# A two-block network on one core: one-hots made in fours and scaled by ScalarE, row products spaced wider, V gathers issued later, attention by pairs of heads

## The chip, the cores and the metric

The kernel runs on one core of a Trainium2 chip. The metric is the device time of one execution in microseconds, the median of three runs. One more execution was taken by the hardware profiler; its trace has the start and duration of every instruction on the engines (PE is TensorE's products, PEld its weight loads, DVE VectorE, ACT ScalarE, POOL GpSimd, SP SyncE, which issues most transfers), each transfer, and the clock that TensorE was granted.

## The reference

Two blocks on 512 tokens of width 1024, all in float32. The first mixes tokens (a gated delta rule and dilated attention) and then applies a PEER layer; the second has two layers, each with a mixer of three kinds (gated linear attention, neighbourhood attention, sliding-window attention, the last two also over 256 context tokens) and a SwiGLU. What the change touches is PEER and the two softmax attentions:

```python
def peer_ffn(xn, w_q, sub_keys, expert_u, expert_v):
    scores = einsum('thcd,hckd->thck', (x2 @ w_q)..., sub_keys)      # 8 heads, 2 halves, 128 keys
    sv, si = top_k(scores, 16)
    cv, ci = top_k(sv[..., 0, :, None] + sv[..., 1, None, :], 16)    # of 256 pairs
    experts = i1 * 128 + i2                                          # 128 experts a token, of 16384
    gates = softmax(cv)
    act = gelu(einsum('tkd,td->tk', expert_u[experts], x))
    return einsum('tk,tkd->td', act * gates, expert_v[experts])
...
s = concat([q k_loc^T * scale + bias, q k_ctx^T * scale (, sink)])   # 6 heads of 64 in each attention
o = softmax(s) @ concat([v_loc, v_ctx])
```

## The kernel before, in words

**Exact products.** Most products are made of three passes over operands split in two parts (`mm3`, L204 to L206: hi x hi, hi x lo, lo x hi). A weight tile of 128 x 1024 is loaded by SP (tile wr), its high part is made by ScalarE (wh, L142), its low part by VectorE (wl, L199). Other products are plain float32; the trace shows each as two records.

**PEER in two ways.** For 384 of the 512 tokens the layer is computed densely: H = gelu(x U^T) for all 16384 experts, in 128 blocks of 24 products of 384 columns (`peer_h`, tile h, stored to DRAM as Hd); a matrix G of gates for every expert and token, made from one-hots (`peer_g`, stored as Gd); then the output as (H * G) V, in 128 blocks of 18 products of 512 columns (`peer_v`). For the first 128 tokens, rows are gathered instead: `sparse_u` gathers a row of U for each of 128 expert places (GpSimd, 128 rows of 4 KB at a time, into a ring of six buffers, four of them slices of x) and VectorE makes the row product (L931), four gathers ahead; when all 128 are there and the gates are known, gelu and gates are applied and the result is transposed; then `sparse_v` gathers rows of V, four gathers a step, 32 steps, each with eight products of 32 weight columns in four column strips (L956).

**G.** A G step (`peer_g`) treats four tokens. One VectorE instruction makes the one-hots of the first key for all four (tile oa, two buffers). For the second key, one VectorE instruction a token compares and multiplies by the gate (L993, tile ob, four buffers of one token). A product a token (L995) gives its 128 x 128 gates in a quarter of a PSUM bank, ScalarE copies the bank to gs. There are 96 G steps.

**The order of the work.** `interleave` writes the instructions of several lanes in one order. It keeps a planned time; each lane yields a pair (planned TensorE time, wait until it is due again), or a condition. The first lane that is due goes next; a spare lane (here `peer_h`, in half-blocks of planned 2.1 us, always due) fills when none is. The order so written is the priority; the framework then places instructions on each engine, and may put a ready one before one whose operands are late. During the selection the lanes are `peer_select` (top 16 of scores, of pairs, and the look-up of indices, nearly all VectorE) and `sparse_u` (a gap of 1.7 a row product). Then, under the mark H+G, `peer_g` (0.9, 1.5) and the first 12 turns of `sparse_v` (2.0, 12.0; one turn is the wait for the row products, so 11 steps). What is left of H follows, and then the V stage with the rest of `sparse_v` beside the dense blocks (4.1, 0). The buffers of the first two V blocks are in a pool that is open from the start; the others use room that the H stage gives back.

**Attention.** In `mixers` the lanes are GLA, three lanes that take attention units from a queue, and the projections. A unit (`attn_unit`) is one head and 128 queries: scores to PSUM, softmax over VectorE and ScalarE (L386 to L396), four or five transposes (two in the context mixer), a copy to SBUF, and the product with V (L410) of 64 weight columns into the head's half of the partitions. `softmax` and `probs_times_v` pause twice a unit (3.2 and 0.9). The mixer runs for the context of the first layer (256 tokens) and for the tokens of both layers (512 each); a further one for the context of the second layer has no attention.

Of the kernel before, what the change touches and what calls it, by code (L numbers as in the profile page):

```python
# [23 lines left out]
CTX = 256  # L24
# [81 lines left out]
class Net:  # L106
# [812 lines left out]
    def sparse_u(s, S):  # L919
# [6 lines left out]
        for k in range(128 + 4):  # L926
            if k < 128:
                ahead.append(s.gather(S, s.I["Ur"], S["rows"][:, k:k + 1]))
            if k >= 4:
                g = ahead.pop(0)  # L930
                nc.vector.tensor_tensor_reduce(g, g, S["xt"], scale=1.0, scalar=0.0, op0=ALU.mult, op1=ALU.add,  # L931
                                               accum_out=act[:, k - 4:k - 3])
                yield 0.0, 1.7
# [8 lines left out]
    def sparse_v(s, S):  # L942
# [7 lines left out]
        for t in range(32):  # L950
# [8 lines left out]
            yield 2.0, 12.0  # L959
# [65 lines left out]
    def peer_hg(s, st, x, Hd, Gd, S, keep):  # L1025
# [27 lines left out]
        with ExitStack() as t:  # L1053
# [134 lines left out]
    def gla(s, p, T, L, pair, s0, sout, y):  # L1188
# [9 lines left out]
        for d in range(2):  # L1198
# [21 lines left out]
            if y is not None:  # L1220
                qin = s.t(p, "gqi", [128, T], 1)
# [90 lines left out]
    def attn_unit(s, p, q, loc, ctx, sink, vs, po, after=None):  # L1312


        mm = s.nc.tensor.matmul
        lw = loc[2] if loc else 0
        b0 = s.bank()
        cps = b0[:, lw:lw + CTX] if lw + CTX <= 512 else s.bank()[:, :CTX]
        segs = [(cps, s.zero[:, 0:1].to_broadcast([128, CTX]), lw)]
        if loc:  # L1320
            mm(b0[:, :lw], q, loc[0], start=True, stop=False)  # L1321
            mm(b0[:, :lw], q, loc[1], start=False, stop=True)
            segs.append((b0[:, :lw], loc[3](), 0))
        mm(cps, q, ctx[0], start=True, stop=False)
        mm(cps, q, ctx[1], start=False, stop=True)
        pr = s.t(p, "pr", [128, 640], 3)
        s.softmax(pr, segs, sink)
        yield (lw + CTX) * 2 * COL, 3.2
        yield from s.probs_times_v(p, pr, vs, po())
        if after:  # L1330
            after()

    def layer_consts(s, p, i):
        s.glan, s.sink = s.t(p, "glan", [128, 16], 1)[:, :2], s.t(p, "sink", [128, 16], 1)[:, :6]
# [35 lines left out]
    def mixers(s, st, i, T, xp, xh, xl, y, is_ctx, lanes=()):  # L1370
# [9 lines left out]
        def units(kind, n, make):  # L1380
# [36 lines left out]
        def na_units(pair, ks, vw, qs, ck):  # L1417
            def mk(po, after):
                for n in range(nt):
                    nb = None  # L1420
                    if not is_ctx:
                        nb = {}
                    for h in range(2):
                        hh = slice(64 * h, 64 * h + 64)
                        cv = [KV["nv"][:, j, pair * 128 + 64 * h:pair * 128 + 64 * h + 64] for j in range(2)]
                        o = lambda n=n, hh=hh: po()[hh, n * 128:(n + 1) * 128]
                        q = qs[h][:, n * 128:(n + 1) * 128]
                        if is_ctx:
                            yield s.attn_unit(p, q, None, ks[h], None, cv, o, after)
                            continue  # L1430
                        w0 = (0, 64, 192, 256)[n]

                        def bias(n=n, h=h, nb=nb):
                            if "t" not in nb:
                                nb["t"] = s.t(p, "nbias", [128, 2, 256], 2)
                                nc.sync.dma_start(nb["t"], s.I["nabias"][i, n, :, 2 * pair:2 * pair + 2, :])
                            return nb["t"][:, h]
                        vs = [vw[:, n, j, hh] for j in range(2)] + cv
                        yield s.attn_unit(p, q, (ks[h][0][:, w0:w0 + 256], ks[h][1][:, w0:w0 + 256], 256, bias),
                                          ck[h], None, vs, o, after)  # L1440
            return mk

        def swa_units(pair, ks, vt, qs, ck):
            def mk(po, after):
                for n in range(nt):
                    for h in range(2):
                        head = 2 * pair + h
                        kv = head // 3
                        hh, vh = slice(64 * h, 64 * h + 64), slice(64 * kv, 64 * kv + 64)
                        cv = [KV["sv"][:, j, vh] for j in range(2)]  # L1450
                        q = qs[h][:, n * 128:(n + 1) * 128]
                        o = lambda n=n, hh=hh: po()[hh, n * 128:(n + 1) * 128]
                        sk = s.sink[:, head:head + 1]
                        if is_ctx:
                            yield s.attn_unit(p, q, None, ks[kv], sk, cv, o, after)
# [3 lines left out]
                        yield s.attn_unit(p, q, (ks[kv][0][:, lo * 128:hi * 128], ks[kv][1][:, lo * 128:hi * 128], w,  # L1459
                                                 lambda c0=c0, w=w: s.c2["swam"][:, c0:c0 + w]), ck[kv], sk,  # L1460
                                          [vt[:, j, vh] for j in range(lo, hi)] + cv, o, after)
# [4 lines left out]
        def proj_lane():  # L1466
            for kind, m in seq:
# [3 lines left out]
                if kind in ("nk", "sq") and y is not None:  # L1471
                    left = aq.put_pairs - 2
                    yield lambda left=left: aq.done >= left * 2 * nt
# [48 lines left out]
                elif kind == "nq":  # L1522
                    pair = m - 9
                    qs = s.q_parts(p, s.evac(p, ps, "ra", T, bufs=2, scale=0.125, grid=not is_ctx), T, "qp")
                    units(kind, 2 * nt, dict(units=na_units(pair, A["k"], A["v"], qs, A.get("ck")),
# [425 lines left out]
```

## Time and profile before

| | us |
|---|---|
| median of three runs (4079.09 to 4084.34) | 4083.6 |
| profiled execution, its own time | 4080.38 |
| its span, first to last instruction | 4078.6 |
| TensorE busy | 3921.0 (96%) |
| VectorE busy | 2324.0 (57%) |
| ScalarE busy | 1573.6 (39%) |
| GpSimd busy | 325.7 (8%) |

The kernel moves 637.62 MB, 156 GB/s over the span; in the PEER part it is near 300. The mean granted clock is 0.988. In lists of groups the columns are line, engine, operation, tiles, shapes, count, busy time, mean ns of one, idle time of the engine before them and what ended it. Busy times of TensorE overlap, as a product starts before the one ahead of it ends.

### The profile page before, as it was taken

What the parts mean: (1) busy time and instruction counts of PE and PEld (TensorE: products, weight loads), DVE (VectorE), ACT (ScalarE), POOL (GpSimd) and SP (SyncE); (2) the same over time, 40 slices, a digit from 0 to 9 for tenths busy, and PEclk for the clock granted to TensorE, in tenths of its full rate; (3) what the DMA queues carried; (4) which work ended last, traced back from release to release, by engine and by line L of the source; (5) the groups of instructions that cost most, each with busy time, mean ns of one, the idle gap of its engine ahead of it and who ended that gap; (6) DMA issues with size and microseconds to landing.
All of it is one profiled execution on the core that took longest, in us unless ns stands there. A gap on an engine that the chain in (4) does not pass through costs nothing.

```text
span 4078.6 us, 57929 instructions
## 1 busy us (share of the span) xinstructions
PE 3921.0 (96%) x22491; PEld 3316.5 (81%) x22491; DVE 2324.0 (57%) x5133; ACT 1573.6 (39%) x2776; POOL 325.7 (8%) x287
## 2 busy tenths in 40 slices
PE   8999999999878999989998999999999999999998
PEld 5878988789877899766887778888888888887887
DVE  7526544569998776434556757663222266664334
ACT  5335454433223333323333645553121245553222
POOL 0000000004445310222000000000000000000000
PEclk9999999999998999999999999999999999999999
DMA  5342132338889876988764651121212141122332
GB/s 196 106 150 74 37 99 98 113 115 321 316 293 326 319 266 236 339 287 308 257 217 163 241 198 43 58 83 63 67 63 62 60 127 58 55 86 78 95 96 83
DMA packets 218594, 637.62 MB, mean 156 GB/s; under 512 B 25552, under 2 KB 65360, under 8 KB 214736
## 3 DMA queue, kind: packets, MB, share of 16 engines
q1 hardware_dynamic: 181456, 499.69, 36.3%
q0 software_dynamic: 36864, 134.23, 9.1%
q8 instruction: 177, 2.90, 0.3%
q14 instruction: 97, 0.79, 0.1%
HBM read 575.12 MB, written 58.72 MB: 155 GB/s over the span
## 4 chain that ended last, share of the span: by engine, by line
PE 54%; DMA 8%; DVE 6%; issue 1%; ACT 1%; POOL 0%; DVEq 0%; SPq 0%; ACTq 0%; POOLq 0%
PE ac L205 13%; PE ac L206 13%; PE ac L204 13%; DMA pa<-Hd 6%; PE po L410 3%; PE bk L995 2%; DVE wl L199 2%; PE bk L236 2%; PE bk L205 1%; PE bk L204 1%; PE bk L206 1%; DVE pl L145 1%; DMA wr<-V 1%; PE bk L1321 1%; PE bk L1165 1%
## 5 line engine op out<-in xcount | busy, mean ns | idle before, releaser
L204 PE MATMUL ac<-xh,wh 128*128 128x512 f32 (+2 forms) x3608 | 1301.6, 362 | 54.2 <-ACT h L136 41.2
L206 PE MATMUL ac<-xh,wl 128*128 128x512 f32 (+2 forms) x3608 | 1280.8, 356 | 14.1 <-DVE wl L199 13.8
L205 PE MATMUL ac<-xl,wh 128*128 128x512 f32 (+2 forms) x3608 | 1282.0, 356 | 1.0 <-DVE xl L148 0.7
L142 ACT ACTIVATE wh<-wr 128x1024 fp32r<-128x1024 f32 (+1 forms) x599 | 630.4, 1054 | 1618.9 <-PE ac L205 1173.4
L199 DVE TENSOR_TENSOR wl<-wr,wh 128x1024 fp32r<-128x1024 f32 (+1 forms) x599 | 726.9, 1214 | 557.4 <-ACT wh L142 529.8
L204 PEld LDWEIGHTS ac<-xh,wh 128*128 128x128 f32 x3608 | 683.8, 190 | 160.5 <-ACT h L136 51.7
L206 PEld LDWEIGHTS ac<-xh,wl 128*128 128x128 f32 x3608 | 683.8, 190 | 96.4 <-DVE wl L199 20.7
L205 PEld LDWEIGHTS ac<-xl,wh 128*128 128x128 f32 x3608 | 684.7, 190 | 79.8 <-issue 7.8
L145 DVE TENSOR_TENSOR pa<-pa,pg 128x384 f32<-128x384 f32 x128 | 66.1, 555 | 298.1 <-DMA pa<-Hd 292.0
L205 PE MATMUL bk<-wl,ph 128*128 128x512 f32 x512 | 201.2, 393 | 0.0
L204 PE MATMUL bk<-wh,ph 128*128 128x512 f32 x512 | 201.1, 393 | 0.0
L206 PE MATMUL bk<-wh,pl 128*128 128x512 f32 x512 | 200.6, 392 | 0.0
L205 PE MATMUL ac<-al,wh 128*128 128x512 f32 (+1 forms) x528 | 186.0, 352 | 0.0
L206 PE MATMUL ac<-ah,wl 128*128 128x512 f32 (+1 forms) x528 | 185.5, 351 | 0.0
L204 PE MATMUL ac<-ah,wh 128*128 128x512 f32 (+1 forms) x528 | 185.0, 350 | 0.0
L148 DVE SCALAR_TENSOR_TENSOR x<-ac,mod,x 128x512 f32<-128x512 f32 (+1 forms) x64 | 46.4, 726 | 186.1 <-PE ac L206 185.8
L993 DVE TENSOR_SCALAR ob<-iota,pi,pi 128x128 f32<-128x128 f32 x384 | 110.2, 350 | 72.7 <-PE bk L995 70.0
L915 POOL DMA_INDIRECT x<-Ur,rows x86 | 121.5, 1413 | 329.1 <-DVE sc L825 213.1
L145 DVE TENSOR_TENSOR nt<-ac,nt 128x512 f32<-128x512 f32 (+1 forms) x44 | 29.9, 680 | 160.2 <-PE ac L206 159.9
L142 ACT ACTIVATE ph<-pa 128x384 fp32r<-128x384 f32 x128 | 66.7, 523 | 138.8 <-DVE pa L145 61.9
L205 PE MATMUL ac<-wl,ph 128*128 128x512 f32 x256 | 101.9, 398 | 18.7 <-DVE wl L199 18.7
L915 POOL DMA_INDIRECT x<-V,rowsT x86 | 97.0, 1128 | 236.1 <-PE bk L956 212.4
(450 smaller groups left out, 5820.9 us busy)
## 6 DMA issues: line engine op xcount, KB each, us to landing
wr<-win SPq DMA_DIRECT2D x151, 512.0 KB, 3.5
wr<-U SPq DMA_DIRECT2D x128, 512.0 KB, 5.4
wr<-V SPq DMA_DIRECT2D x128, 512.0 KB, 5.8
mw<-wmod SPq DMA_DIRECT2D x96, 512.0 KB, 4.2
Hd<-h SPq DMA_DIRECT2D x64, 384.0 KB, 4.9
pa<-Hd SPq DMA_DIRECT2D x64, 384.0 KB, 5.9
Gd<-gs SPq DMA_DIRECT2D x24, 1024.0 KB, 7.5
pg<-Gd SPq DMA_DIRECT2D x21, 1152.0 KB, 7.2
```

Of the source, the lines that this page charges most:

```text
L142: s.nc.scalar.activation(out, in_, AF.Copy, **kw)
L145: s.nc.vector.tensor_tensor(out, a, b, op=op)
L148: s.nc.vector.scalar_tensor_tensor(out, a, sc, b, op0=op0, op1=op1)
L199: (eng or nc.vector).tensor_tensor(lo[:, :nk, :], raw[:, :nk, :], r32(hi[:, :nk, :]), op=ALU.subtract)
L204: mm(out, ah, bh, start=start, stop=False)
L205: mm(out, ah, bl, start=False, stop=False)
L206: mm(out, al, bh, start=False, stop=stop)
L236: s.nc.tensor.transpose(out, in_, s.ident)
L410: s.nc.tensor.matmul(po, vs[j], pt[:, j, :], start=j == 0, stop=j == nb - 1, skip_group_check=True)
L915: s.nc.gpsimd.indirect_dma_start(out=g, out_offset=None, in_=table, in_offset=bass.IndirectOffsetOnAxis(ap=idx, axis=0))
L993: nc.vector.tensor_scalar(a2, iota, iT[1][:, tok:tok + 1], iT[2][:, tok:tok + 1], op0=ALU.is_equal, op1=ALU.mult)
L995: nc.tensor.matmul(b[:, i * 128:(i + 1) * 128], a1[:, i], a2, start=True, stop=True)
```

## The change

- A G step makes the second one-hots for four tokens in one VectorE instruction too (tile ob, two buffers of four tokens); ScalarE multiplies each token's 128 x 128 by its gate, in place, ahead of the token's product.
- A row product's gap is 2.9 until the gates are known and 4.0 after. The lane of row products ends with the selection, and what is left of them runs as a lane of the H+G stage.
- Of `sparse_v`, 8 turns instead of 12 belong to H+G, and a step's gap is 15.0 instead of 12.0.
- A unit of attention is a pair of heads and 128 queries. The pair's transposes share banks, and the products with V alternate between the heads, so between the two halves of the columns. The output bank is first cleared by one product with zeros. There are two lanes of attention instead of three, and four buffers for probabilities instead of three.
- GLA's scaled q takes the buffer of its log decay; two small constants share a tile.

```diff
@@ sparse_u @@
-                yield 0.0, 1.7
+                yield 0.0, 2.9 if "gated" not in S else 4.0
@@ sparse_v @@
-            yield 2.0, 12.0
+            yield 2.0, 15.0
@@ peer_g @@
+                a2 = s.t(gp, "ob", [128, 4, 128], 2)
+                s.tt(a2, iota[:, None, :].to_broadcast([128, 4, 128]),
+                     iT[1][:, t0:t0 + 4, None].to_broadcast([128, 4, 128]), ALU.is_equal)
                 for i in range(4):
-                    tok = t0 + i
-                    a2 = s.t(gp, "ob", [128, 128], 4)
-                    nc.vector.tensor_scalar(a2, iota, iT[1][:, tok:tok + 1], iT[2][:, tok:tok + 1],
-                                            op0=ALU.is_equal, op1=ALU.mult)
-                    nc.tensor.matmul(b[:, i * 128:(i + 1) * 128], a1[:, i], a2, start=True, stop=True)
+                    s.copy(a2[:, i], a2[:, i], scale=iT[2][:, t0 + i:t0 + i + 1])
+                    nc.tensor.matmul(b[:, i * 128:(i + 1) * 128], a1[:, i], a2[:, i], start=True, stop=True)
@@ peer_hg @@
-            su, sv = s.sparse_u(S), s.sparse_v(S)
-            interleave([s.peer_select(p, sc, iota, iT, S), su], hs)
+            su, sv, last = s.sparse_u(S), s.sparse_v(S), []
+            def while_selecting():
+                yield from s.peer_select(p, sc, iota, iT, S)
+                last.append(True)
+            def dots():
+                yield lambda: "chosen" in S
+                while not last and "gated" not in S:
+                    yield next(su)
+            interleave([while_selecting(), dots()], hs)
...
-            interleave([s.peer_g(gp, iota, iT, Gd), s.until(sv, 12)], hs)
+            interleave([s.peer_g(gp, iota, iT, Gd), su, s.until(sv, 8)], hs)
@@ gla @@
-                qin = s.t(p, "gqi", [128, T], 1)
+                qin = s.t(p, "gla", [128, T], 1)
@@ attn_unit becomes attn_pair @@
+    def attn_pair(s, p, heads, po, after):
+        mm = s.nc.tensor.matmul
+        prs = []
+        for q, loc, ctx, sink, vs in heads:
...
+            pr = s.t(p, "pr", [128, 640], 4)
+            s.softmax(pr, segs, sink)
+            prs.append(pr)
+            yield (lw + CTX) * 2 * COL, 1.0
+        yield 0.0, 2.2
+        nb = len(heads[0][4])
+        out = po()
+        for j0 in range(0, nb, 2):
+            js = range(j0, min(nb, j0 + 2))
+            b = s.bank()
+            pt = s.t(p, "pt", [128, 4, 128], 3)
+            n = 2 * len(js)
+            for j in js:
+                for h in range(2):
+                    c = 2 * (j - j0) + h
+                    s.transpose(b[:, c * 128:(c + 1) * 128], prs[h][:, j * 128:(j + 1) * 128])
+            s.copy(flat(pt[:, :n, :]), b[:, :n * 128])
+            yield n * 0.11, 0.9
+            for j in js:
+                for h in range(2):
+                    mm(out[64 * h:64 * h + 64], heads[h][4][j], pt[:, 2 * (j - j0) + h, :], start=False,
+                       stop=j == nb - 1, skip_group_check=True)
+            yield n * 0.13, 0.0
+        after()
@@ units, po @@
                     box["b"] = s.pob()
+                    nc.tensor.matmul(box["b"][:, :T], s.zero.bitcast(F32R), make["some"], start=True, stop=False,
+                                     skip_group_check=True)
@@ proj_lane @@
-                    yield lambda left=left: aq.done >= left * 2 * nt
+                    yield lambda left=left: aq.done >= left * nt
@@ mixers @@
-        interleave([gq.lane(), aq.lane(), aq.lane(), aq.lane(), *lanes, proj_lane()])
+        interleave([gq.lane(), aq.lane(), aq.lane(), *lanes, proj_lane()])
```

## Rows read from the trace of the kernel before

**Rows 1.** By stretch: us, busy PE PEld DVE ACT POOL, clock, DMA, GB/s.
```profile
895.00:1310.00 415.00, 359.00 (x1936) 342.87 (x1935) 398.94 (x1096) 123.64 (x171) 184.78 (x134) 0.97 0.87 307
1310.00:1598.00 288.00, 288.00 (x1955) 269.48 (x1955) 212.78 (x535) 112.61 (x180) 49.82 (x44) 0.99 0.75 273
1616.00:1945.00 329.00, 307.77 (x1444) 221.49 (x1441) 137.53 (x210) 100.97 (x132) 86.78 (x78) 0.98 0.87 310
1945.00:2198.00 253.00, 250.28 (x1102) 206.28 (x1101) 128.49 (x183) 95.69 (x123) 0.00 (x0) 1.00 0.68 230
...
2460.00:2710.00 250.00, 246.53 (x1619) 205.07 (x1618) 166.65 (x505) 141.66 (x294) 0.00 (x0) 1.00 0.18 55
```
**Rows 2.** Timeline of TensorE in H+G: start us, us, engine, line, operation, tiles, shapes.
```profile
1519.55 0.42 PE L204 MATMUL ac<-xh,wh 128*128 128x384 f32 x1
...
1519.99 0.34 PE L206 MATMUL ac<-xh,wl 128*128 128x384 f32 x1
...
1521.73 1.05 PE L995 MATMUL bk<-ob,oa 128*128 128x128 f32 x8
1522.54 0.42 PE L204 MATMUL ac<-xh,wh 128*128 128x384 f32 x1
```
**Rows 3.** Groups of TensorE, 895 to 1310 us.
```profile
L204 PE MATMUL ac<-xh,wh 128*128 128x384 f32 x641 | 223.0, 348 | 41.3 <-ACT h L136 41.2
L206 PE MATMUL ac<-xh,wl 128*128 128x384 f32 x642 | 220.5, 344 | 11.0 <-DVE wl L199 10.7
```
**Rows 4.** Timeline of TensorE in the V stage, around one V-row step.
```profile
1678.76 0.39 PE L205 MATMUL bk<-wl,ph 128*128 128x512 f32 x1
...
1679.67 0.39 PE L206 MATMUL bk<-wh,pl 128*128 128x512 f32 x1
...
1681.84 0.50 PE L204 MATMUL ac<-wh,ph 128*128 128x512 f32 x1
```
**Rows 5.** Groups of VectorE, 895 to 1310 us.
```profile
L931 DVE CUSTOM_DVE_ANT_0 x<-x,sxt 128x1024 f32<-128x1024 f32 x86 | 104.0, 1211 | 8.5 <-DMA x<-Ur,rows 8.5
L199 DVE TENSOR_TENSOR wl<-wr,wh 128x1024 fp32r<-128x1024 f32 x80 | 97.2, 1214 | 0.0
```
**Rows 6.** Groups of VectorE, 1310 to 1598 us.
```profile
L993 DVE TENSOR_SCALAR ob<-iota,pi,pi 128x128 f32<-128x128 f32 x382 | 109.6, 350 | 72.7 <-PE bk L995 70.0
L145 DVE TENSOR_TENSOR oa<-iota,pi 128x512 f32<-128x512 f32 x95 | 65.2, 686 | 0.0
```
**Rows 7.** Groups of ScalarE, 1310 to 1598 us.
```profile
L142 ACT ACTIVATE gs<-bk 128x512 f32<-128x512 f32 x96 | 57.1, 595 | 120.6 <-PE bk L995 118.4 <-issue 2.2
L142 ACT ACTIVATE wh<-wr 128x1024 fp32r<-128x1024 f32 x42 | 44.4, 1058 | 55.8 <-PE ac L205 55.8
L136 ACT ACTIVATE h<-ac 128x384 f32<-128x384 f32 x42 | 19.9, 474 | 0.0
```
**Rows 8.** A group of ScalarE, 2460 to 2710 us.
```profile
L142 ACT ACTIVATE pt<-bk 128x128 f32<-128x128 f32 x12 | 3.3, 272 | 0.0
```
**Rows 9.** Timeline of GpSimd and TensorE at the border of H and V.
```profile
1616.51 0.94 POOL L915 DMA_INDIRECT sr<-V,rowsT  x1 [145.74 <-PE bk L956]
...
1627.96 0.62 PE L956 MATMUL po<-sr,sw 128*32 128x512 f32 x1 [2.34 <-DMA sr<-V,rowsT]
...
1634.60 0.50 PE L204 MATMUL ac<-wh,ph 128*128 128x512 f32 x1 [2.29 <-ACT ph L142]
...
1651.28 0.62 PE L956 MATMUL po<-x,sw 128*32 128x512 f32 x2
```
**Rows 10.** Timeline of TensorE in the first layer's long mixer.
```profile
2521.86 1.09 PE L1271 MATMUL bk<-gat,gvt 128*64 128x128 f32 x16
2522.89 0.66 PE L236 MATMUL bk<-ident,pr 128*128 128x128 f32 x4
...
2595.82 0.65 PE L410 MATMUL po<-pt,svt 128*64 128x128 f32 x4
...
2596.84 0.39 PE L1321 MATMUL bk<-nkh,qp 128*128 128x256 f32 x1
```

More of the change, by code (lines that the diff above doesn't have):

```diff
@@ L1310, in k_parts @@
         return out
-    def attn_unit(s, p, q, loc, ctx, sink, vs, po, after=None):
+    def attn_pair(s, p, heads, po, after):
         mm = s.nc.tensor.matmul
[L1316 to L1331, printed above, removed]
+        prs = []
+        for q, loc, ctx, sink, vs in heads:
+            lw = loc[2] if loc else 0
+            b0 = s.bank()
+            cps = b0[:, lw:lw + CTX] if lw + CTX <= 512 else s.bank()[:, :CTX]
+            segs = [(cps, s.zero[:, 0:1].to_broadcast([128, CTX]), lw)]
+            if loc:
+                mm(b0[:, :lw], q, loc[0], start=True, stop=False)
+                mm(b0[:, :lw], q, loc[1], start=False, stop=True)
+                segs.append((b0[:, :lw], loc[3](), 0))
+            mm(cps, q, ctx[0], start=True, stop=False)
+            mm(cps, q, ctx[1], start=False, stop=True)
+            pr = s.t(p, "pr", [128, 640], 4)
[22 more added lines that the diff above has]
+        after()
@@ L1419, in mk, with bias @@
                 for n in range(nt):
-                    nb = None
-                    if not is_ctx:
-                        nb = {}
+                    nb, w0 = {}, (0, 64, 192, 256)[n]
+                    def bias(h, n=n, nb=nb):
+                        if "t" not in nb:
+                            nb["t"] = s.t(p, "nbias", [128, 2, 256], 2)
+                            nc.sync.dma_start(nb["t"], s.I["nabias"][i, n, :, 2 * pair:2 * pair + 2, :])
+                        return nb["t"][:, h]
+                    heads = []
                     for h in range(2):
@@ L1425, in mk @@
                         cv = [KV["nv"][:, j, pair * 128 + 64 * h:pair * 128 + 64 * h + 64] for j in range(2)]
-                        o = lambda n=n, hh=hh: po()[hh, n * 128:(n + 1) * 128]
                         q = qs[h][:, n * 128:(n + 1) * 128]
                         if is_ctx:
-                            yield s.attn_unit(p, q, None, ks[h], None, cv, o, after)
+                            heads.append((q, None, ks[h], None, cv))
                             continue
[L1431 to L1440, printed above, removed]
+                        loc = (ks[h][0][:, w0:w0 + 256], ks[h][1][:, w0:w0 + 256], 256, lambda h=h, b=bias: b(h))
+                        heads.append((q, loc, ck[h], None, [vw[:, n, j, hh] for j in range(2)] + cv))
+                    yield s.attn_pair(p, heads, lambda n=n: po()[:, n * 128:(n + 1) * 128], after)
             return mk
@@ L1445, in mk @@
                 for n in range(nt):
+                    heads = []
                     for h in range(2):
@@ L1448, in mk @@
                         kv = head // 3
-                        hh, vh = slice(64 * h, 64 * h + 64), slice(64 * kv, 64 * kv + 64)
+                        vh = slice(64 * kv, 64 * kv + 64)
                         cv = [KV["sv"][:, j, vh] for j in range(2)]
                         q = qs[h][:, n * 128:(n + 1) * 128]
-                        o = lambda n=n, hh=hh: po()[hh, n * 128:(n + 1) * 128]
                         sk = s.sink[:, head:head + 1]
                         if is_ctx:
-                            yield s.attn_unit(p, q, None, ks[kv], sk, cv, o, after)
+                            heads.append((q, None, ks[kv], sk, cv))
                             continue
@@ L1458, in mk @@
                         c0, w = (lo - n + 1) * 128, (hi - lo) * 128
-                        yield s.attn_unit(p, q, (ks[kv][0][:, lo * 128:hi * 128], ks[kv][1][:, lo * 128:hi * 128], w,
-                                                 lambda c0=c0, w=w: s.c2["swam"][:, c0:c0 + w]), ck[kv], sk,
-                                          [vt[:, j, vh] for j in range(lo, hi)] + cv, o, after)
+                        loc = (ks[kv][0][:, lo * 128:hi * 128], ks[kv][1][:, lo * 128:hi * 128], w,
+                               lambda c0=c0, w=w: s.c2["swam"][:, c0:c0 + w])
+                        heads.append((q, loc, ck[kv], sk, [vt[:, j, vh] for j in range(lo, hi)] + cv))
+                    yield s.attn_pair(p, heads, lambda n=n: po()[:, n * 128:(n + 1) * 128], after)
             return mk
@@ L1547, in proj_lane @@
                     qs = s.q_parts(p, src, T, "qp")
-                    units(kind, 2 * nt, dict(units=swa_units(pair, A["sk"], A["sv"], qs, A.get("sck")),
+                    units(kind, nt, dict(units=swa_units(pair, A["sk"], A["sv"], qs, A.get("sck")), some=A["sk"][0][0],
                                              out=out_plain(5 + pair)))
```

9 lines of the change are left out of this document (5 added, 4 removed).

## The prediction

> **What bounds the kernel now.** I read the page's table of engines first: TensorE is busy 96% of the span, so only a stage in which it waits, or in which its own work shrinks, can give time. Then the engines by stretch [rows 1], for the stages that the change touches. In 895 to 1310 us (selection of the experts beside the dense H products) VectorE is busy 399 of 415 us while TensorE loses time. How much is not its idle time, since pipelined products overlap; I take work at its pace instead. Ten products of an H block start 0.174 us apart (1519.99 to 1521.73), so a block of 24 costs 4.17 us [rows 2]; the stretch holds 641 + 642 products of two of the three kinds and as many of the third [rows 3], 80 blocks, 334 us. TensorE lost 81 us of 415, and what it waits for is ScalarE's h and VectorE's wl [rows 3], both behind the full VectorE. In 1310 to 1598 (H with G) the granted clock is 0.99 and I find no loss to speak of: half a block and a G step take 2.99 us together (1519.55 to 1522.54), 2.18 and 0.81 [rows 2]. In the V stage (1616 to 2198) 128 blocks of 18 products, 0.2275 us apart (four of them 1678.76 to 1679.67), cost 4.09 us each = 524, and 21 of the 32 V-row steps 1.94 us each (1679.90, where the last product's turn ends, to 1681.84) = 41 [rows 4]: 565 of 582 us, 17 lost. In the long mixer (2460 to 2710; the second layer's, 3400 to 3655, is the same program) TensorE is busy 246.5 of 250 us [rows 1].
>
> **How the written order changes.** H is the spare lane, in half-blocks of 2.1 planned us; another lane gets its turn at the first half boundary after its due time. A gap of 1.7 gives one row product per half, two per block. A gap of 2.9 runs to the second boundary: one per block. Selecting for one tile of 128 tokens has twelve steps of gap 2.4 or 2.6 (4.2 each) and four pairs of 1.6 and 2.6 (2.1 + 4.2): 75.6 planned us = 18 blocks, so four tiles and the gates take 74 blocks. Before, the 128 row products (from block 18 on, two per block) outlast the selection and end at block 82; the trace has the two stages' border there (80 blocks in the stretch, two ahead of it). After, the selection ends at block 74 with 56 row products written. Left for H+G: 54 blocks, 96 G steps, 72 row products. Two G steps and two halves advance the plan by 6.0, and the gap of 4.0 again gives one row product per block: 54. So **18 row products are written behind the last H block**, and behind them the gates' product, V-row steps 0 to 6 of the H+G stage and step 7 of the V stage, before any V block. Before, 11 V-row steps lay inside H+G.
>
> **Selection.** VectorE sets its end. It loses 72 row products of 1.21 us, 87 us, and 8 weight splits of 1.214, 10 us [rows 5]: 415 - 97 = 318 us. TensorE's 72 blocks there need 300, so VectorE stays the bound, narrowly; I add 4 us: 322, **-93 us**. Bounds: 300 (VectorE never ends last) and 340 (as much loss per block as in a half of today's).
>
> **H+G.** 8 more blocks at 4.36 us = +35, and 11 V-row steps less = -21. VectorE: a G step's second one-hot was four of 350 ns, now one of 0.686 like the first [rows 6]; 96 x 2 x 0.686 + 54 x 1.214 + 72 x 1.21 = 284 us of about 313, so it has room even for the 18 late row products. ScalarE: 96 x 0.595 + 54 x (1.058 + 0.474) = 140 [rows 7] + 384 scaled copies. No row has a 128x128 copy scaled by a column; the nearest are 272 ns for a plain one from PSUM [rows 8] and 350 ns, VectorE's instruction that it replaces [rows 6]. I take 272: 104 us, 134 at the upper end; 244 to 274 of 313. ScalarE is strictly in order, and gs and h wait there for TensorE, so copies can come late. What hides that is room: both one-hots have two buffers of four tokens, and today VectorE waits for TensorE there (70.0 us [rows 6]), so it runs ahead. I take 8 us, bounds 0 and 82 (rival B). Sum **+22 us**.
> The Trainium skill, "ScalarE: Activation LUTs", section "What ACT_TABLE_LOAD costs", states 186 ns + 0.833 ns per column, 93 more for each operand by pointer and 93 of overlap back to back. By it a scaled copy would last 386 ns and take 293 of the engine, 112 us in all (an estimate from that page). It speaks against the move more than the 272 ns row does, and the sum would stay the same, as ScalarE would still be under TensorE.
>
> **Border and V stage.** The 11 V-row steps come back: +21 us. At the border, row products and V-row steps have no H to hide them. A V-row step needs four gathered buffers of a ring of six: issued from 1616.51 on, the last product to wait started at 1627.96 [rows 9], 11.4 us a step while DMA is loaded. Against that, two V blocks have their own early pool (8.2 us of cover), VectorE's room lets waiting row products move forward, and the trace shows V blocks placed in the middle of a V-row step (from 1634.60, the step's rest at 1651.28 [rows 9]): the order is not kept where an operand is late. I take 18 us of new loss, between 0 and 99 (rival A). Further on, a V-row step comes after four blocks instead of three: transfers per step are 4 x 0.92 + 2.1 MB (V, Hd and Gd of a block; four gathers of 128 x 1024 x 4 bytes) in 18.3 us = 316 GB/s, against 4.85 MB in 14.2 = 341 before; the stretch with both ran at 310 GB/s [rows 1], at the wall. I take -4 us (0 to -17). Sum **+35 us**. In H+G the rate goes from 273 GB/s [rows 1] by 72 x 0.52 MB / 313 us (+120) and 11 x 2.1 MB / 288 us (-80) to some 313, about what the stretches beside it move; the moved gathers then stand on POOL's queue with no V gather before them and share the transfer engines with U's weights on SP's, which I leave inside the 8 us. PEER together: -93 + 22 + 35 = **-36 us**.
>
> **Attention by pairs.** Probabilities times V is 8 or 10 records of 64 columns in a row for a head, all in one column half: eight start within 1.02 us (2595.82 to 2596.84), 0.127 each. GLA's product of the same shape alternates the halves: sixteen in 1.03 us (2521.86 to 2522.89), 0.064 each [rows 10]. Now both heads alternate so. The 408 records of a long mixer save 0.063 each = 25.7 us, less six opening products of 0.23 = 1.4; the context mixer (96 records) 5.4: 54 us where TensorE is the bound. Against it: two lanes of pairs instead of three of heads, with four pauses or five instead of two per unit. In the plan of a long mixer 22 heads are left after the last projection instead of 14, and its idle time rises from 7 to 33 us (with planned product times below the traced ones), so two pairs in flight cover a softmax chain less well. I take 9 us off in each long mixer and 4 in the context one: **-32 us**; bounds -54 and +25 (the plan's 26 us more in either, less half of the gain). qin in la's buffer can delay the next direction's la, but only if nothing else is ready, and projections are: nothing, up to 10 us if not (four vector and scalar steps of 0.6 us, four directions). The merged constants and one more pr buffer: nothing either way.
>
> **Sum.** -36 - 32 = -68 us on the profiled run of 4080.4, which is 3 us under the median shown: 4012 to 4015; **4014 us**.
>
> **Rivals.**
> A, the uncovered border (slower): 18 row products at VectorE's 1.21 and some wait = 23 us, eight V-row steps at 11.4 - 1.9 = 76; 99 us instead of 18: 4095. It turns the change from 86 us on. For: the written order, a ring of six, slow gathers under load. Against: V blocks can be placed between, row products early.
> B, late copies in G: where copies stand behind h on ScalarE, each block waits h 0.47 + a copy 0.27 + hops, some 1.0 us, and 0.7 more behind gs and wh in its other half: 48 x 1.7 = 82 instead of 8: 4088. For: one strict queue. Against: two buffers, VectorE ahead today.
> C, two lanes starve attention: nothing or +10 instead of -32: 4046 to 4056. For: the plan's idle time. Against: the next projection (the output's) can fill in.
> D, all of it: border 5, G 0, attention -50, the rest as summed: 3975.
>
> **Chances.** Forecast as worked out (3985 to 4045) 0.48; D 0.12; C 0.12; part of A or B (up to 4075) 0.06; B 0.11; A 0.11. Range 3965 to 4090. A measurement tells about 0.2%, 8 us, from no change: faster 0.78 (the first four), same 0.08 (most of B), slower 0.14 (A and the rest of B).
>
> **What would show it.** The first G product near 1217 us, not 1310; VectorE over 95% busy until then; H ending near 1535; the V-row products' first wait for gathers right behind it, and how many V blocks stand among them; no long wait of L995's products for ScalarE's copies; probabilities times V at 0.064 us a record, and each long mixer about 15 us shorter. Wrong if TensorE waits over 60 us between the last H and the third V block, if a G step with half a block takes over 3.7 us, or if the mixers keep their length.

## The result, and the profile after

The changed kernel takes 4039.2 us (median of four runs, 4036.4 to 4043.5) against 4082.9 for the kernel before in the same session: ratio 0.9895, 95% interval 0.9878 to 0.9912. It is 43.7 us faster; 68 were forecast. The profiled executions stand 36.8 us apart (spans 4041.8 and 4078.6), and they can be compared stage by stage. I put the borders at the first G product, the last H product, the last dense V product and the first score product of each long mixer:

```
us by stage              before   after   change  forecast
start to first G         1309.7  1228.8   -80.9     -93
first G to last H         304.7   308.1    +3.4     +22
last H to last V          602.8   661.2   +58.4     +35
last V to long mixer 1    258.3   248.9    -9.4      -1.4
long mixer 1 to 2         940.6   937.0    -3.6     -15.3
long mixer 2 to the end   662.4   657.7    -4.7     -15.3
sum                                      -36.8     -68
```

The sign held, the sizes did not: two terms came out better than forecast and four worse. Two causes, which the experiments settle, carry most of the misses: V-row steps cut into pieces behind H, and too few attention units in flight. First the same views as before, of the changed kernel.

By stretch, columns as in [rows 1] (selection; H with G; the 109 us behind the last H; the rest of the V stage; the first long mixer):

```profile
895.00:1229.00 334.00, 318.53 (x1772) 310.61 (x1772) 323.43 (x966) 112.93 (x158) 109.56 (x75) 0.98 0.80 274
1229.00:1537.00 308.00, 308.00 (x2034) 307.29 (x2034) 247.66 (x366) 240.21 (x589) 84.46 (x59) 1.00 0.83 313
1537.00:1646.00 109.00, 103.09 (x345) 43.83 (x344) 30.62 (x52) 20.56 (x27) 41.00 (x39) 0.97 0.92 324
1646.00:2198.00 552.00, 535.21 (x2473) 406.54 (x2473) 246.23 (x365) 177.71 (x232) 88.67 (x83) 0.99 0.77 271
2447.00:2678.00 231.00, 220.51 (x1560) 176.95 (x1559) 158.15 (x491) 133.05 (x274) 0.00 (x0) 0.98 0.17 54
```

In the selection VectorE is still full, 323 of 334 us, but TensorE loses far less. Its waits there (what it waited for: us in all, times, longest) answer to [rows 3], where the waits for h and wl were 41.2 and 10.7 us:

```profile
PE bk L236 <- DVE pi L892: 11.1, 3, 6.1
PE ac L206 <- DVE wl L199: 2.8, 6, 1.6
PE ac L204 <- ACT h L136: 1.2, 2, 0.9
```

The first line is new: three transpositions of expert indices wait for VectorE's copy of the ones before them, 6.1 us at 1088 us and 4.1 at 1169, so the full VectorE now holds TensorE up there.

Groups of VectorE in the same stretch, to set beside [rows 5]: 47 + 22 = 69 row products stand in the selection, where I had 56.

```profile
L931 DVE CUSTOM_DVE_ANT_0 x<-x,sxt 128x1024 f32<-128x1024 f32 x47 | 57.1, 1225 | 5.0 <-DMA x<-Ur,rows 5.0
L931 DVE CUSTOM_DVE_ANT_0 sr<-sr,sxt 128x1024 f32<-128x1024 f32 x22 | 26.9, 1225 | 1.2 <-DMA sr<-Ur,rows 1.2
```

In H with G the new scaled copies lead ScalarE's groups, and VectorE's one-hots of four tokens its own; these answer to [rows 6, 7]:

```profile
L142 ACT ACTIVATE ob<-ob,pi 128x128 f32<-128x128 f32 x383 | 124.9, 394 | 30.4 <-DVE ob L145 30.3
L142 ACT ACTIVATE wh<-wr 128x1024 fp32r<-128x1024 f32 x54 | 56.7, 1051 | 15.1 <-PE ac L205 12.2 <-DMA wr<-V 2.6 <-issue 0.2
L142 ACT ACTIVATE gs<-bk 128x512 f32<-128x512 f32 x96 | 56.4, 588 | 20.2 <-PE bk L995 20.1
```
```profile
L145 DVE TENSOR_TENSOR ob<-iota,pi 128x512 f32<-128x512 f32 x95 | 64.9, 683 | 0.0
L145 DVE TENSOR_TENSOR oa<-iota,pi 128x512 f32<-128x512 f32 x94 | 64.6, 687 | 39.1 <-PE bk L995 39.0
```

A copy lasts 394 ns, not the 272 of my row [rows 8], and still no G product waits: TensorE is busy 308 of 308 us, and VectorE waits for TensorE (39.0 us), not the other way round.

The unforeseen thing is in the V stage. The timeline of TensorE (start, us, engine, line, tiles, shapes, count of records) 36 us behind the last H product:

```profile
1572.48 0.40 PE L205 MATMUL bk<-wl,ph 128*128 128x512 f32 x1
1572.81 1.06 PE L956 MATMUL po<-x,sw 128*32 128x512 f32 x4
1573.69 1.04 PE L956 MATMUL bk<-x,sw 128*32 128x512 f32 x4
1574.66 0.50 PE L206 MATMUL bk<-wh,pl 128*128 128x512 f32 x1
1574.99 0.40 PE L204 MATMUL ac<-wh,ph 128*128 128x512 f32 x1
1575.23 0.39 PE L205 MATMUL ac<-wl,ph 128*128 128x512 f32 x1
...
1576.24 1.04 PE L956 MATMUL po<-sr,sw 128*32 128x512 f32 x2
1577.12 1.02 PE L956 MATMUL bk<-sr,sw 128*32 128x512 f32 x2
1578.07 0.50 PE L206 MATMUL bk<-wh,pl 128*128 128x512 f32 x1
...
1579.91 1.04 PE L956 MATMUL po<-sr,sw 128*32 128x512 f32 x2
1580.79 1.02 PE L956 MATMUL bk<-sr,sw 128*32 128x512 f32 x2
1581.74 0.50 PE L204 MATMUL bk<-wh,ph 128*128 128x512 f32 x1
```

One V-row step is eight products on four column strips of 32, two on each strip; each product leaves two records. Here the step comes in three pieces of 8, 4 and 4 records (two strips, then one, then one), and between them stand six or seven dense V products. From its first start to the next full-width start a piece lasts 1574.66 - 1572.81 = 1.85 us, 1578.07 - 1576.24 = 1.83 and 1581.74 - 1579.91 = 1.83: the same with two strips in it or one. A whole step of 16 records lasts 1.85 us too (in v_all_later, below). So the two products of one strip run one after the other, and those of different strips side by side where they follow each other directly; across the dense products between two pieces they do not. Cut in three, a step costs 5.5 us instead of 1.85. TensorE waits for next to nothing meanwhile (103 of 109 us busy in the stretch from 1537), so neither its busy share nor its waits show the loss. The count of instructions does: 345 in 109 us, where the same stretch behind the last H of the kernel before has 495 with the same busy time:

```profile
1616.00:1725.00 109.00, 103.75 (x495) 73.68 (x491) 47.51 (x72) 35.91 (x47) 30.41 (x28) 1.00 0.96 347
```

The Trainium skill, "TensorEngine Tiling (Array Packing)", section "Key Properties", says that a change of tiling mode drains the engine. The trace fits that, and shows that it is the small part: full-width products start 0.24 us apart (1574.99 to 1575.23), and 0.33 at either edge of a piece (1572.48 to 1572.81, 1574.66 to 1574.99), some 0.2 us for both; the two more pieces cost 3.65 us a step.

In the long mixers pairs run as forecast only in part. Groups of TensorE in the first one, for [rows 10]: the record's mean hides the spacing, so I add up from each start to the next over all 408 records: 51.2 us before (0.125 each), 33.5 after (0.082; 0.064 forecast). And TensorE now waits for the softmax (the probabilities pr), 7.1 us where 2.7 were (first line: the kernel before, 2460 to 2699 us; the others: after):

```profile
PE bk L236 <- DVE pr L396: 2.7, 4, 1.8
PE bk L236 <- DVE pr L396: 7.1, 5, 2.3
PE po L1360 <- ACT pt L142: 1.0, 3, 0.4
```

Twice, behind such a wait, the granted clock is low for a stretch (1.2 GHz for most of it; columns as above):

```profile
2634.00:2642.00 8.00, 6.62 (x35) 4.91 (x35) 4.12 (x14) 4.47 (x10) 0.00 (x0) 0.57 0.22 66
2675.00:2684.00 9.00, 6.94 (x40) 5.82 (x38) 4.25 (x7) 4.98 (x9) 0.00 (x0) 0.62 0.23 69
```

### The profile page after: what moved, and what is told of

Same layout as the page of the kernel before. It is cut to its first block, busy times and chain, and to the rows that moved or that the text cites. A ratio compares the mean times of both kernels' runs of the same rounds, so it can differ in the third digit from the quotient of the medians.

```text
span 4041.8 us, 58180 instructions
## 1 busy us (share of the span) xinstructions
PE 3909.7 (97%) x22509; PEld 3272.3 (81%) x22509; DVE 2282.9 (56%) x4845; ACT 1679.0 (42%) x3136; POOL 328.0 (8%) x287
## 4 chain that ended last, share of the span: by engine, by line
PE 75%; DVE 13%; DMA 7%; issue 3%; ACT 2%; POOL 0%; SPq 0%; DVEq 0%; ACTq 0%; POOLq 0%
PE ac L204 18%; PE ac L205 18%; PE ac L206 18%; DMA pa<-Hd 6%; DVE wl L199 4%; PE bk L236 3%; PE bk L995 2%; PE po L1360 2%; PE bk L1175 1%; PE bk L204 1%; PE bk L205 1%; PE bk L206 1%; PE bk L561 1%; PE bk L555 1%; DVE pl L145 1%
## 5 line engine op out<-in xcount | busy, mean ns | idle before, releaser
L206 PE MATMUL bk<-wh,pl 128*128 128x512 f32 x512 | 201.4, 393 | 0.0
L142 ACT ACTIVATE ob<-ob,pi 128x128 f32<-128x128 f32 x384 | 125.1, 393 | 30.4 <-DVE ob L145 30.3
```

The costliest lines, as they stand in the source:

```text
L142: s.nc.scalar.activation(out, in_, AF.Copy, **kw)
L206: mm(out, al, bh, start=False, stop=stop)
```

## The experiments

Each has five to seven executions, with the kernel before beside them (its medians in four sessions: 4084.6, 4084.9, 4083.3, 4081.4). Ratios and intervals are against the kernel before; differences are against the changed kernel's 4039.2 unless another is named.

**The two halves, each alone.** peer_only keeps the changed PEER with the attention of the kernel before, attn_only the reverse.

```diff
 # peer_only: mixers as before
-        interleave([gq.lane(), aq.lane(), aq.lane(), *lanes, proj_lane()])
+        interleave([gq.lane(), aq.lane(), aq.lane(), aq.lane(), *lanes, proj_lane()])
...
 # attn_only: PEER as before
-                yield 0.0, 2.9 if "gated" not in S else 4.0
+                yield 0.0, 1.7
...
-            interleave([s.peer_g(gp, iota, iT, Gd), su, s.until(sv, 8)], hs)
+            interleave([s.peer_g(gp, iota, iT, Gd), s.until(sv, 12)], hs)
```

> The PEER half of the change alone (one-hots, gaps, V gathers), attention as before. Theory from the two traces: up to the end of the V stage the changed kernel gained 19 us of 37, so this one should be at 4061 to 4067 (ratio 0.9945 to 0.996). Rival, the forecast's shares (36 us from PEER, the rest lost elsewhere by chance of placement): 4045 to 4050.

> The attention half alone (pairs of heads, two lanes), PEER as before. Theory from the traces: context mixer -9 us, each long mixer -4 us, so 4063 to 4068, with records of probabilities times V at 0.06 to 0.08 us where projections fill the waits, and TensorE waiting for the softmax after the last projection. Rival: the halves interact (the mixer's gain is held back by what PEER leaves on the queues), then this one alone gains the forecast's 32 us, 4051.

peer_only: 4052.0 us, ratio 0.9927 (0.9910 to 0.9944), -32.5: between the two expectations, and nearer to the forecast's -36. The theory missed by 9 us because it was read from the changed kernel's profile, whose V stage is 12.5 us longer than peer_only's, though both place it alike. attn_only: 4067.3, 0.9961 (0.9947 to 0.9975), -17.3, as the trace had it. Together -49.8 for the measured -43.7, so the halves hardly touch each other: the 6 us between the two sums are less than one V stage varies (below). PEER's half came close to its forecast sum, by errors that cancel (below); attention gave half of its.

**The cut steps: v_all_later and dots_sooner.** The first writes no V-row step beside H and G; the second keeps eight there and spaces the row products of H with G closer.

```diff
 # v_all_later
-            interleave([s.peer_g(gp, iota, iT, Gd), su, s.until(sv, 8)], hs)
+            interleave([s.peer_g(gp, iota, iT, Gd), su], hs)
...
 # dots_sooner
-                yield 0.0, 2.9 if "gated" not in S else 4.0
+                yield 0.0, 2.9
```

> The changed kernel with one edit: no V-row step belongs to the H+G stage, so all 32 come after four V blocks each and none stand in a row at the border. Theory 1 (pieces): at the border the placed order cuts nine V-row steps into single products between V products, so that the four column strips no longer run side by side and a step costs about 7 us instead of 1.9; without the pieces the V stage gets 30 to 40 us shorter: 4000 to 4010. Theory 2 (gathers): the border is slow because gathers and V weights share transfers at 313 GB/s; the bytes are the same, so nothing is gained: 4034 to 4042.

> The changed kernel with one edit: a row product's gap is 2.9 in H+G too, which comes to one for each half-block instead of one for each block, so they end within H+G and 7 V-row steps find H blocks to lie between. Theory 1 (pieces): 4000 to 4010, with the steps whole again. Theory 2 (gathers at the wall): 4034 to 4042. Rival to both: VectorE gets full in H+G (two row products, two G steps and a split are 6.4 us for a block of 6.0) and the stage grows by 10 to 20 us: 4015 to 4025.

v_all_later: 4006.0 us, 0.9815 (0.9798 to 0.9832), 33 us better, as theory 1 has it. All but two of its steps run as one piece; TensorE's timeline around one:

```profile
1600.02 0.39 PE L206 MATMUL bk<-wh,pl 128*128 128x512 f32 x1
1600.34 0.62 PE L956 MATMUL po<-x,sw 128*32 128x512 f32 x2
1600.35 0.62 PE L956 MATMUL po<-sr,sw 128*32 128x512 f32 x2
...
1601.65 0.60 PE L956 MATMUL bk<-x,sw 128*32 128x512 f32 x2
1601.66 0.60 PE L956 MATMUL bk<-sr,sw 128*32 128x512 f32 x2
1602.19 0.51 PE L204 MATMUL ac<-wh,ph 128*128 128x512 f32 x1
```

The strips start 0.01 us apart, and the eight products take 1602.19 - 1600.34 = 1.85 us. By stretch, the 109 us behind its last H hold as many instructions as before, 480:

```profile
1535.00:1644.00 109.00, 103.57 (x480) 74.42 (x480) 49.07 (x77) 37.01 (x50) 26.08 (x24) 0.98 0.88 312
```

dots_sooner: 4018.7, 0.9839 (0.9821 to 0.9856). This is outside theory 1 and inside the range of the rival to both, but not for the rival's reason: VectorE is busy 248 of 319 us in H with G. Six steps stand whole there and lengthen it by 12 us; behind it two are still cut, and one dense product waits 9.6 us for ph (the high part of H * G, made by ScalarE). A whole step costs the same on either side of the border, so nothing is won by having some early.

**Dose: v4 and v_before.** Four turns of `sparse_v` instead of eight are written beside H and G, or twelve with the old gap (one turn is the wait for the row products, so they are three, seven and eleven steps).

```diff
 # v4
-            interleave([s.peer_g(gp, iota, iT, Gd), su, s.until(sv, 8)], hs)
+            interleave([s.peer_g(gp, iota, iT, Gd), su, s.until(sv, 4)], hs)
...
 # v_before
-            interleave([s.peer_g(gp, iota, iT, Gd), su, s.until(sv, 8)], hs)
+            interleave([s.peer_g(gp, iota, iT, Gd), su, s.until(sv, 12)], hs)
...
-            yield 2.0, 15.0
+            yield 2.0, 12.0
```

> The changed kernel with four V-row steps instead of eight written beside H and G. Theory (each step written there is placed at the border cut into single products between dense products, so that its four column strips no longer run side by side, about 7.2 us for a step against 1.94 us whole): four cut steps fewer, 4 x 5.3 = 21 us, so 4014 to 4023. Rival (the border is slow because the rows of V come late over the queue): fewer steps written early bring no row sooner, 4035 to 4050.

> The changed kernel with twelve V-row steps written beside H and G and a gap of 12.0, as the kernel before has them. Theory of the cut steps: four more cut steps, 4 x 5.3 = 21 us, so 4055 to 4065. Rival (it is the later issue of the gathers that costs the V stage its 23 us over the forecast): the earlier issue gives it back, 4015 to 4030.

v4: 4024.6 us, 0.9839 (0.9821 to 0.9858), 1.6 us above the theory's range and far from the rival's. v_before: 4063.8, 0.9945 (0.9932 to 0.9959), inside it. The traces carry the size of one cut. I counted the steps that stand in pieces of 8, 4 and 4 records in each V stage, summed the V-row products from start to next start, and took off 1.85 us for every step:

```
                  turns written  steps  V-row us over  dense V   V stage
                  beside H, G      cut    1.85 a step       us        us
v_all_later             0           0            9.2     556.7     624.4
v4                      4           4           14.6     569.7     642.9
changed kernel          8           9           34.6     568.0     661.2
v_before               12          17           64.8     560.9     684.3
kernel before          12           0            8.7     556.0     602.8
```

Each cut step costs 3.65 us (two more pieces), at every dose: 4 make 14.6 us, 9 make 32.9 and 17 make 62.1. What is left, 1.7 and 2.7 us, is pieces that last longer than 1.85, and the 9 us of the two kernels without cut steps stand mostly in one place, a run of 22 records behind H that waits for a gathered row (4.1 us of waiting in v_all_later). The cutting goes on beyond the steps written early: twelve turns hold 11 steps, and 17 are cut. So the expectations met v_before's time partly by luck: they reckoned with four more cut steps at 5.3 us, and it was eight at 3.65. v_before also has the closer gap, so its time alone does not separate the two; the column of V-row products does.

The kernel before also writes twelve turns, but its row products are done before G begins, so eleven steps run whole inside H and G and 21 remain for its V stage. The dense products spread over 14 us without following the dose: peer_only has the same pieces in its V stage as the changed kernel and 555.2 us of dense products there, against 568.0; 8 us of the difference are TensorE's waits for wl (8.6 and 16.7 us). Most likely that is chance between executions: peer_only's six lie in two groups, 4047 to 4048 and 4056 to 4058 us, and the profiled one is of the first. It bounds what one profile can tell of this stage.

**The one-hots: old_ob.**

```diff
-                a2 = s.t(gp, "ob", [128, 4, 128], 2)
-                s.tt(a2, iota[:, None, :].to_broadcast([128, 4, 128]),
-                     iT[1][:, t0:t0 + 4, None].to_broadcast([128, 4, 128]), ALU.is_equal)
                 for i in range(4):
-                    s.copy(a2[:, i], a2[:, i], scale=iT[2][:, t0 + i:t0 + i + 1])
...
+                    tok = t0 + i
+                    a2 = s.t(gp, "ob", [128, 128], 4)
+                    nc.vector.tensor_scalar(a2, iota, iT[1][:, tok:tok + 1], iT[2][:, tok:tok + 1],
+                                            op0=ALU.is_equal, op1=ALU.mult)
...
```

> The changed kernel with the four one-hot instructions with gates on VectorE (350 ns each) in place of one (about 690 ns) and four ScalarE copies. Theory (H+G of the changed kernel is held by TensorE only because VectorE has room): VectorE's 238 us in 280 grow by 96 x 0.71 = 68 us over the stage's 308, to about 330 us, so the stage grows by at least 22 us: 4058 to 4080. Rival (VectorE has room enough and the one-hots run ahead anyway): 4036 to 4046.

4044.8 us, 0.9908 (0.9893 to 0.9923): the rival, 5.6 us above the changed kernel. H with G grows by 4.3 us only. The window of its G products and VectorE's group in it:

```profile
1229.00:1509.00 280.00, 280.00 (x1846) 276.34 (x1845) 274.14 (x631) 116.67 (x186) 69.49 (x59) 1.00 0.86 315
```
```profile
L993 DVE TENSOR_SCALAR ob<-iota,pi,pi 128x128 f32<-128x128 f32 x372 | 108.2, 352 | 5.1 <-PE bk L995 4.8
```

VectorE goes to 274 of 280 us and just keeps up. My 0.71 us more for each G step came from the mean of 350 ns [rows 6]; but 372 of them occupy 108.2 us, 291 each, since they overlap. At 291 a G step costs 0.48 us more, an estimate of 46 us in all, which makes VectorE's 248 of 308 us 294; the trace has 287 of 312.

**The spacing: later_gap17** (against v_all_later).

```diff
-                yield 0.0, 2.9 if "gated" not in S else 4.0
+                yield 0.0, 1.7 if "gated" not in S else 4.0
```

> v_all_later with the row products of the selection at a gap of 1.7, as the kernel before has them. Theory (the gain of the selection is TensorE's waits for ScalarE's h, which is held up by VectorE full of row products: 41.2 + 10.7 us before, 1.2 + 2.8 after): about 45 us come back, 4040 to 4060. Rival (the row products cost the same wherever they stand, what they leave in the selection they take beside H and G): 4000 to 4015.

4054.1 us, 0.9936 (0.9922 to 0.9949): 48 us come back, as the theory has it. 114 row products stand ahead of the first G instead of 69, it comes at 1281.6 instead of 1227.3 us, and the old waits of TensorE from 895 to 1310 us are there again:

```profile
PE ac L204 <- ACT h L136: 42.6, 28, 4.9
PE ac L206 <- DVE wl L199: 10.7, 11, 1.3
```

So the wider gap is what shortens the selection, and it is the largest gain of the change. Note how little of it the wait names: the engine named is ScalarE, the engine that holds it up VectorE.

**Lanes: lanes3.** Three lanes of pairs, with six tiles for pr instead of four; pt, ra and nbias give the room, one buffer each. The run changes lanes and tiles together.

```diff
-            pr = s.t(p, "pr", [128, 640], 4)
+            pr = s.t(p, "pr", [128, 640], 6)
...
-            pt = s.t(p, "pt", [128, 4, 128], 3)
+            pt = s.t(p, "pt", [128, 4, 128], 2)
...
-        interleave([gq.lane(), aq.lane(), aq.lane(), *lanes, proj_lane()])
+        interleave([gq.lane(), aq.lane(), aq.lane(), aq.lane(), *lanes, proj_lane()])
```

> The changed kernel with three lanes of head pairs instead of two in the mixers (six probability tiles instead of four; for their room two pt tiles instead of three, one ra and one nbias tile instead of two). Theory (two lanes leave TensorE without work while both pairs are in their softmax, waits of 7.4 us and some 14 us at half clock in each long mixer): the third lane covers most of it, 4019 to 4031. Rival (the long mixers gained little because the strip products run at 0.082 us and not 0.064 us and the transposes wait, whatever the lanes): 4036 to 4045.

4009.3 us, 0.9801 (0.9783 to 0.9820): 30 us better, more than the theory had. From its first score product to its last product with V, a long mixer takes 235.4 us before, 231.1 after and 214.6 with three lanes. The first one's window and all of TensorE's waits in it:

```profile
2448.00:2663.00 215.00, 214.12 (x1560) 173.74 (x1559) 156.02 (x492) 132.05 (x275) 0.00 (x0) 1.00 0.19 60
```
```profile
PE po L1360 <- ACT pt L142: 0.3, 1, 0.3
```

The wait for pr is gone, and so is the second loss behind it: the granted clock is 1.00 throughout. The strip products go from 0.082 only to 0.079 us a record (32.1 us), so the rival's price was not the missing part.

**All together: later_lanes3, and two variants of it.** The first joins v_all_later and lanes3; the second puts the old one-hots into it; the third widens the row products' gap in the selection to 4.0 and narrows the V-row steps' from 15.0 to 12.0.

```diff
 # later_lanes3_wide
-                yield 0.0, 2.9 if "gated" not in S else 4.0
+                yield 0.0, 4.0
...
-            yield 2.0, 15.0
+            yield 2.0, 12.0
```

> The changed kernel with no V-row step written beside H and G and with three lanes of head pairs in the mixers (tiles as in lanes3). Theory (the cut steps and the two lanes are two separate losses, in stages that don't touch): 4006 - 30 = 3976, so 3968 to 3984. Rival (what one gives back the other takes, as the weights come no sooner in the V stage and the mixers): 3990 to 4006.

> later_lanes3 with the four gated one-hot instructions on VectorE of the kernel before. Theory (VectorE, nearly full in H+G, still keeps up, as in old_ob): 0 to 6 us over later_lanes3, 3974 to 3984. Rival (the gates on ScalarE carry a part of the gain once the V steps no longer wait at the border): 10 us and more over it, 3986 to 4000.

> later_lanes3 with the row products at a gap of 4.0 in the selection too (about 19 more of them leave it), and V-row steps at a gap of 12.0, since they start later. Theory (VectorE, 97% busy, still sets the end of the selection): 19 x 1.21 = 23 us less there, until TensorE's own 300 to 310 us bind; beside H and G VectorE has the room; 10 to 20 us gained, 3955 to 3966. Rival (the row products that outlast H hold up the V-row steps, and transfers pay for the closer steps): 3972 to 3990.

later_lanes3: 3974.6 us, 0.9736 (0.9722 to 0.9749), the sum of the two to a microsecond or two, and the fastest here: 109 us under the kernel before, 65 under the changed one. With the old one-hots 3984.7, 0.9761 (0.9748 to 0.9775): 10 us more, just above the theory's range and below the rival's. The trace gives H with G 4.6 us of that (312.7 against 308.1), as old_ob did; 8.5 us lie in its V stage (633.8 against 625.3), which is within what that stage varies between profiles, so it stays open whether they belong to the one-hots. The wide one: 3992.2, 0.9783 (0.9769 to 0.9796), slower, and my expectation was wrong in its first half for a reason that stands in the prediction: the half-blocks of H advance the plan by 2.1, so a gap of 4.0 ends at the same boundary as 2.9. The order up to the last H is unchanged (69 row products ahead of G, last H at 1536.0 and 1536.4). What is left is a test of the V gap, and the closer steps cost 17.6 us (17.0 of them in the V stage): TensorE waits 25.9 us for wl there, against 18.7 in later_lanes3, and the 109 us from 1536 move 333 GB/s against 313. That transfers are the cause fits this but was not tested by itself.

## Why the prediction was right, and where its sizes were off

**The bound of the selection: right.** VectorE full, TensorE behind it through h and wl, 97% busy after. The term is 12 us short (-80.9 for -93) because 69 row products stood ahead of the first G and not 56: 13 x 1.22 = 16 us. By the prediction's count of the written order 56 stand there; in the placed order 13 more come early (which of the framework's choices does it was not looked into). By the same step "18 row products behind the last H block" was wrong: the last of the 128 ended at 1399.3 us, in the middle of H with G.

**H with G: mechanism right, size too high** (+3.4 for +22). TensorE did bind. From start to next start, the H products take 230.6 us there instead of 201.4, +29 (52.7 blocks instead of 46; 6 us less than forecast, as the selection, being longer, held one block more); the eleven V-row steps take 22 us with them as forecast; the G products need 77.4 us instead of 81.3, 4 less and not 8 more. Rival B is out: no wait of TensorE for a copy, though the copy lasts 394 ns. The Trainium skill, "ScalarE: Activation LUTs", section "What ACT_TABLE_LOAD costs", had 386 (an estimate from its figures), and the trace agrees with the page rather than with my row; the engine time is 124.9 / 383 = 326 ns each, between the estimate's 293 and 386, since only 245 of the 384 start directly behind another copy, some 0.1 us before that one's end.

**Border and V stage: the mis-sized term** (+58.4 for +35). The forecast saw the place: V-row steps written back to back behind H, four gathers each against a ring of six tiles, V blocks placed in between. It priced a wait for gathers, 18 us, and that wait is 2.8 us. What decided was how the blocks were placed in between: into the steps. The first 24 records, six tiles' worth, run in one piece; from there a step proceeds as tiles come free, 1583.55 - 1572.81 = 10.7 us a step, close to the 11.4 of rival A, with TensorE busy all the while. Its cost is nine steps at 3.65 us, 33 us, a term that the sum did not have: it put V blocks between the products of a step down as cover. The stage's ledger: eleven more steps at 1.85 +20, V-row time over that 34.6 - 8.7 = +26, dense products +12, of which most may be chance. The -4 us for transfers that I took to stand at a wall of 310 GB/s [rows 1] had no such wall: the kernel before moved 347 GB/s in the 109 us behind its last H (the row above). I also read the stage before as ending at 2198 us; its last dense V product ends at 2217, so its loss before was 36 us, not 17, and this left no trace in the sum, as only differences entered it. Rival A is refuted as a wait; its place and pace were right, and what the place did cost is a third of its 99 us, by another mechanism.

**Attention: rival C in part** (-17.6 for -32). The side-by-side products are real (51.2 to 33.5 us, 17.7 of 25.7 in the first long mixer), and the context mixer gave 9.4 us, where I had written most of it off. But the 9 us that I took off each long mixer for two pairs in flight are 16.5 and 16.2, as lanes3 gives them back, and these and the 8 us missing in the strip products cover the 12 us that the first long mixer lacks. Of the signs of being wrong, "if the mixers keep their length" came close: 235.4 us became 231.1. The profile before gave a hint, which I only argue: its heads came three at a time, with 2.7 us of waits left, and a pair takes less of TensorE's time per head while its softmax stays as long.

**The sum.** Selection 12 short, H with G 19 better, V stage 23 worse, attention 14 short: 31 us less than forecast on the profiled runs, 24 by the medians. The range held because the rivals stood in it, not because the terms were good to 10 us; the total lies within 24 us partly by luck, as 19 us too pessimistic in one stage make up for 49 too optimistic in the others.

## What to carry to other kernels

Here products on column strips were worth their price only back to back (1.85 us against 5.5): look in the timeline at whether a group that was written together is placed together, and give it its operands (or write it later) until it is. A busy TensorE can hide such a loss (103 of 109 us busy with 345 instructions where 495 ran before); compare instructions per microsecond in like stretches. When work per unit shrinks, ask again how many units must be in flight to cover the chain between their halves.

## What the runs showed that I had not expected

A piece of a V-row step lasts 1.83 to 1.85 us with one, two or four strips in it. VectorE's 128x128 tensor_scalar has a mean of 352 ns and occupies 291, so a mean from the profile can overstate what a run of like instructions costs by a fifth. A V stage placed alike took 648.7 and 661.2 us in the profiled executions of peer_only and the changed kernel, nearly all of the difference in its dense products, whose waits for the low part of the weights are 8 us longer. That a third lane of pairs, with its tiles, brought more (30 us) than pairs in two lanes (17) was not foreseen either.
